# A hybrid encoder layer on one core: group 1's values and gates as seven block products, its weight sums made in group 0's retention stage, down-projection units 14 and 15 made ahead

## The chip, the core and the metric

The kernel runs on one core of a Trainium2 chip. Its time is the device time of one execution in microseconds (us); the number to compare is the median over several executions. The engines are TensorE (PE: matrix products; PEld is its weight load, which overlaps), VectorE (DVE), ScalarE (ACT), GpSimd (POOL) and SyncE (SP), which issues most of the transfers between DRAM and on-chip memory.

## The reference

One layer is applied to 2048 prompt frames and 8 streams of 16 new frames, all of width 1024. Its two token mixers share one input projection:

```python
p = jnp.einsum('btd,de->bte', x, w_in)
rq, rk, rv, rg, sq, sk, sv = jnp.split(p, PROJ_OFFSETS, axis=-1)
# retention: 4 heads, 128 wide
scores = jnp.einsum('bnhd,bmhd->bhnm', q, k) * dmask
o = jnp.einsum('bhnm,bmhe->bnhe', scores, v)
o = o + jnp.einsum('bnhd,bhde->bnhe', q, s) * q_decay[None, :, :, None]
return (jax.nn.silu(g.astype(jnp.float32)) * on).astype(g.dtype)   # on: o, normalised per head
# window attention: 8 query heads, 2 key heads, 64 wide, a sink in each softmax
p = sink_softmax(s, sinks)
o = jnp.einsum('bcgrqk,bckgd->bcqgrd', p.astype(v.dtype), vb)
# then, with mix = concatenate([retention, window attention])
x = layer_norm(ALPHA * x + jnp.einsum('btm,md->btd', mix, w_out), ln1_w, ln1_b)
h = jnp.square(jax.nn.relu(jnp.einsum('btd,df->btf', x, w_up)))
return layer_norm(ALPHA * x + jnp.einsum('btf,fd->btd', h, w_down), ln2_w, ln2_b)
```

The change concerns the columns `rv` and `rg` (values and gates of retention, 512 each) for six of the token tiles. Everything is computed to float32 accuracy.

## The kernel before

**Tiles, groups, stages.** The tokens stand in 17 tiles of 128, in three groups: group 0 has tiles 0 to 4, group 1 tiles 5 to 10, group 2 the sample tile and tiles 11 to 15. The groups run one after the other, each through stages whose names end the names of all buffers: keys and values of window attention (`1kv` for group 1), retention queries and keys (`1qk`; in group 0 a stage `0sq` instead), retention (`1ret`: values, gates, the recurrence), the output projection (`1out`) and the MLP (`1mlp`).

**Products.** [...] A product takes three matmuls: high by high, low by high, high by low. Where a weight is made into such a pair on the chip, ACT casts the high part (L297) and DVE subtracts to get the low part (L313).

**Seven block products.** Many projections go by a scheme of Strassen's kind: tokens are taken in pairs of half-blocks (three pairs of tiles in a group of six), the weight in 2 x 2 blocks, and seven products of sums of blocks stand for eight. Products are called 11, 12, 22 and S1 to S4; S1 to S4 of the weights are sums of weight blocks, T1 to T4 are the sums of the tokens that they meet (T2 meets S2, T1 meets S1, T3 meets S3, and T4 meets 22). Results are put together by DVE additions from PSUM. Before, queries and keys go this way in groups 1 and 2, values and gates (vg) only in group 2: `VGT = (2,)` at L54. In group 1 each of six tiles meets both halves of the 1024 value and gate columns directly: 2 x 6 x 8 slices x 3 = 288 matmuls of 128x512.

**The weight sums of vg.** `vg_operands` (L708) loads four blocks of the raw weight at a time, makes four sums on DVE (128x256 each), casts them on ACT, subtracts on DVE, and stores them in DRAM, in eight rounds. Before, it starts in group 1's MLP once that is past its first pair of units, one sum in 8 us. `vg_units` (from L2440) runs the seven products, in the order 11, 12, S2, S3, 22, S1, S4 (L413), with the stored sums reloaded as weights.

**The token sums.** `sums_task` (L1110) makes T1 to T4 for queries and keys. Where vg uses the seven products too, `store_sum` (L1092) saves T1 and T2 in DRAM before their room is given away, and `again_task` (L1101) reloads them in the retention stage.

**Down projection.** It has 16 units, used in pairs in the MLP. Group 0 makes their operands in place. For groups 1 and 2 `right_operands` (L756) can make units ahead and store them (kept_d), in the order 0, 1, 14, 15, 2, 3 and on; what isn't made ahead is made directly inside group 1's MLP (`direct_operand` L865, `direct_unit` L878), which also stores it for group 2. In this kernel units 0, 1, 14 and 15 are made ahead.

**Window attention.** `swa_task` (L1320) takes the prompt tiles of a group one by one: scores on TensorE, softmax on DVE and ACT, transposes of the probabilities on TensorE, copies, and the weighted sum on TensorE. In groups 1 and 2 the tiles from the fourth on go first. The output stage uses a tile's mix only when this is done; its units are taken by L2371 in the order of tiles 0, 3, 4, 5, 1, 2 for the first half of the columns in group 1.

**What sets the order.** The program is written by a planner (`Sched`, L58). Each piece of work is a generator that yields the time at which it wants to go on; a table of costs gives each engine's time, and TensorE's products are emitted in turn, with the pieces put between them as they come due. `idle("DVE", slack)` waits until the planner has DVE free; `room(tag, n)` waits for free buffers of a pool (14 of xT, 10 of w, 4 of raw, 20 of y, 8 of u3, 2 of st). So a change in one stage moves the order around it. Once written, the order on each engine is fixed. Transfers are issued by SP in the program's order, and each piece waits on semaphores for its inputs.

Of the kernel before, what the change touches and what calls it, by code (L numbers as in the profile page):

```python
# [11 lines left out]
ALU = mybir.AluOpType  # L12
# [41 lines left out]
VGT = (2,)  # L54
# [125 lines left out]
def tile_layer(ctx: ExitStack, tc: tile.TileContext, A: dict, O: dict):  # L180
# [527 lines left out]
    def vg_operands():  # L708

        while at_pair[0] < 1.0 or ph[0] != "1mlp":  # L710
            yield S.now + 1.0
# [8 lines left out]
        due = 0.0  # L720
        for n_ in range(8):
            kt, i = n_ // 2, n_ % 2
            while not room("y", 3):
                yield S.now + 0.3
            src = [take("y", [P, 2, 256]) for _ in range(2)]
# [4 lines left out]
            yield S.ready(*src) + 1.5  # L730
            a11, a12, a21, a22 = [src[x // 2][:, x % 2, :] for x in range(4)]
            for o, t, args in (("S1", a22, (a21, a22, ALU.add)), ("S3", a21, (a11, a21, ALU.subtract)),
                               ("S2", a11, (a22, a11, ALU.subtract)), ("S4", a12, (a12, a11, ALU.subtract))):
                while not room("y") or S.now < due:
                    yield S.now + 0.3
                due = S.now + 8.0
                hl = take("y", [P, 512], F32R)
                yield max(S.ready(*src, eng="DVE"), S.fence[hl.tensor.name])
                yield from idle("DVE", QUIET)
                vtt(t, *args)  # L740
                yield S.ready(t, eng="ACT")
                acopy(hl[:, 0:256], t)
                yield S.ready(hl[:, 0:256], eng="DVE")
                vtt(hl[:, 256:512], t, hl[:, 0:256].bitcast(F32), ALU.subtract)
                stored.append(S.add(save(kt, i, o, hl)))
# [10 lines left out]
    def right_operands():  # L756
# [43 lines left out]
        for n_, j in enumerate((0, 1, max(STR) - 2, max(STR) - 1) + tuple(range(2, max(STR) - 2))):  # L800
# [291 lines left out]
    def store_sum(o, hl, norms):  # L1092
        while not all(t[3] for t in norms):
            yield S.now + 0.5
        yield S.ready(*hl, eng="SP") - 0.3
        for k, t in zip(kept_t[o], hl):
            dma(k, t.bitcast(F32))

    norms = []
# [222 lines left out]
    def swa_task(tiles, slot, sq_tasks, qTs, kTall, vall, mixs, after=()):  # L1322
# [4 lines left out]
        if after:  # L1327
            todo.sort(key=lambda x: x[0] < 3)
# [732 lines left out]
    for gi, tiles in enumerate(GROUPS):  # L2061
# [102 lines left out]
        def qk_units(gi):  # L2164
# [40 lines left out]
            X = {"11": (0, 0), "12": (0, 1), "S4": (1, 1)}  # L2205
            for o, h in qk_order(gi):
                hs = [h_ for o_, h_ in qk_order(gi) if o_ == o]
# [587 lines left out]
        if not gi:  # L2795
            S.add(right_operands())
            if VGT:
                S.add(vg_operands())
# [192 lines left out]
```

## Time and profile before

| what | before |
|---|---|
| median of 3 runs | 2244.03 us (2242.72 to 2244.43) |
| profiled execution | 2241.79 us, span 2240.0 us |
| TensorE busy | 2221.1 us of the span |
| DVE busy | 1636.8 us |
| ACT busy | 1021.9 us |
| group 1: qk, retention, output | 95.13, 109.30 and 79.45 us |
| group 0: retention | 157.69 us |
| group 1: MLP | 467.71 us |

The stages' bounds are the first matmuls of TensorE whose results bear the stage's name. In rows of the profile, `out<-in` are buffers by the program's names with their numbers left out, L278 is the matmul helper, L284 the transposes, L297 ACT's copies and casts, L313 DVE's additions and subtractions, L359 the transfers. The time in brackets at a row's end is idle time before it, with the engine and the buffer that ended it.

### The profile page before, as it was taken

What the parts mean: (1) busy time and instruction counts of PE and PEld (TensorE: products, weight loads), DVE (VectorE), ACT (ScalarE), POOL (GpSimd) and SP (SyncE); (2) the same over time, 40 slices, a digit from 0 to 9 for tenths busy, and PEclk for the clock granted to TensorE, in tenths of its full rate; (3) what the DMA queues carried; (4) which work ended last, traced back from release to release, by engine and by line L of the source; (5) the groups of instructions that cost most, each with busy time, mean ns of one, the idle gap of its engine ahead of it and who ended that gap; (6) DMA issues with size and microseconds to landing.
All of it is one profiled execution on the core that took longest, in us unless ns stands there. A gap on an engine that the chain in (4) does not pass through costs nothing. (4 is left out here: it accounts for less than half of the span.)

```text
span 2240.0 us, 34600 instructions
## 1 busy us (share of the span) xinstructions
PE 2221.1 (99%) x12149; PEld 1969.8 (88%) x12149; DVE 1636.8 (73%) x3564; ACT 1021.9 (46%) x2407; POOL 95.8 (4%) x131
## 2 busy tenths in 40 slices
PE   9999999999999999999999999999999999999998
PEld 7788889999999988789999999899778999999987
DVE  6767689787877587787788887796775955555567
ACT  5544645555545555473344443366343732222222
POOL 0000000000000001000000000000000000000002
PEclk9999999999999999999999999999999999999999
DMA  7645758999989836767899998999655577777776
GB/s 263 213 169 211 284 197 306 319 327 341 322 311 352 289 130 221 258 247 252 286 338 333 334 336 302 330 346 354 237 172 183 178 254 256 249 252 257 254 255 179
DMA packets 228830, 598.91 MB, mean 267 GB/s; under 512 B 23216, under 2 KB 80304, under 8 KB 228656
## 3 DMA queue, kind: packets, MB, share of 16 engines
q1 hardware_dynamic: 223472, 587.26, 74.8%
q0 software_dynamic: 5184, 9.44, 2.5%
q8 instruction: 96, 1.57, 0.3%
q14 instruction: 78, 0.64, 0.1%
HBM read 401.25 MB, written 185.86 MB: 262 GB/s over the span
## 5 line engine op out<-in xcount | busy, mean ns | idle before, releaser
L278 PE MATMUL sw_1mlp<-xT_1out,w_1mlp 128*128 128x384 f32 x1152 | 209.2, 335 | 0.0
L278 PE MATMUL sw_2mlp<-xT_2out,w_2mlp 128*128 128x384 f32 x1140 | 206.8, 335 | 0.3 <-DVE kvln_2mlp L313 0.3
L278 PEld LDWEIGHTS sw_1mlp<-xT_1out,w_1mlp 128*128 128x128 f32 x1152 | 202.2, 188 | 4.1 <-DMA w_1mlp<-kept 0.5
L278 PEld LDWEIGHTS sw_2mlp<-xT_2out,w_2mlp 128*128 128x128 f32 x1140 | 200.0, 188 | 4.2 <-DVE kvln_2mlp L313 0.6
L278 PE MATMUL sw_0mlp<-xT_0out,w_0mlp 128*128 128x320 f32 x1188 | 179.1, 309 | 0.0
L278 PEld LDWEIGHTS sw_0mlp<-xT_0out,w_0mlp 128*128 128x128 f32 x1188 | 176.5, 188 | 2.2
L278 PE MATMUL rt_2mlp<-w_2mlp,u_2mlp 128*128 128x512 f32 (+1 forms) x522 | 127.1, 388 | 0.0
L278 PE MATMUL rt_1mlp<-w_1mlp,u_1mlp 128*128 128x512 f32 x516 | 126.8, 391 | 0.0
L278 PE MATMUL rt_0mlp<-w_0mlp,u_0mlp 128*128 128x512 f32 x492 | 121.3, 392 | 1.5 <-DVE u_0mlp L313 1.4
L278 PE MATMUL mm_2mlp<-w_2mlp,u_2mlp 128*128 128x512 f32 (+1 forms) x504 | 122.5, 388 | 0.0
L278 PE MATMUL mm_1mlp<-w_1mlp,u_1mlp 128*128 128x512 f32 x492 | 121.2, 391 | 0.0
L278 PEld LDWEIGHTS rt_2mlp<-w_2mlp,u_2mlp 128*128 128x128 f32 x522 | 96.9, 188 | 19.0
L278 PEld LDWEIGHTS rt_1mlp<-w_1mlp,u_1mlp 128*128 128x128 f32 x516 | 96.5, 188 | 19.2
L278 PE MATMUL mm_0mlp<-w_0mlp,u_0mlp 128*128 128x512 f32 x456 | 112.0, 392 | 0.0
L278 PEld LDWEIGHTS rt_0mlp<-w_0mlp,u_0mlp 128*128 128x128 f32 x492 | 92.2, 189 | 20.8 <-DVE u_0mlp L313 1.9
L278 PEld LDWEIGHTS mm_2mlp<-w_2mlp,u_2mlp 128*128 128x128 f32 x504 | 93.6, 188 | 18.4
L278 PEld LDWEIGHTS mm_1mlp<-w_1mlp,u_1mlp 128*128 128x128 f32 x492 | 92.0, 188 | 18.3
L278 PEld LDWEIGHTS mm_0mlp<-w_0mlp,u_0mlp 128*128 128x128 f32 x456 | 85.6, 189 | 17.2
L313 DVE TENSOR_TENSOR w_1mlp<-w_1mlp,w_1mlp 128x512 fp32r<-128x512 f32 (+1 forms) x120 | 81.7, 686 | 14.9 <-ACT w_1mlp L297 14.0
L313 DVE TENSOR_TENSOR w_0mlp<-raw_0mlp,w_0mlp 128x512 fp32r<-128x512 f32 (+1 forms) x69 | 63.5, 921 | 34.8 <-ACT w_0mlp L297 18.9
L297 ACT CAST u_2mlp<-kvln_2mlp 128x384 fp32r<-128x384 f32 x51 | 26.2, 515 | 117.7 <-PE mm_2mlp L278 52.1
L297 ACT CAST w_1mlp<-w_1mlp 128x512 fp32r<-128x512 f32 x84 | 52.0, 619 | 50.1 <-PE sw_1mlp L278 40.1
(1007 smaller groups left out, 4814.3 us busy)
## 6 DMA issues: line engine op xcount, KB each, us to landing
w_1mlp<-kept SPq DMA_DIRECT2D x104, 512.0 KB, 5.4
w_2mlp<-kept SPq DMA_DIRECT2D x102, 512.0 KB, 4.0
w_2mlp<-keptd SPq DMA_DIRECT2D x98, 512.0 KB, 4.2
kept<-w_0mlp SPq DMA_DIRECT2D x96, 512.0 KB, 5.1
keptd<-w_1mlp SPq DMA_DIRECT2D x84, 512.0 KB, 4.4
keptq<-y_0mlp SPq DMA_DIRECT2D x72, 256.0 KB, 5.1
w_1qk<-keptq SPq DMA_DIRECT2D x34, 512.0 KB, 5.7
w_2qk<-keptq SPq DMA_DIRECT2D x34, 512.0 KB, 6.2
```

The lines of the kernel that those rows point to most:

```text
L278: S.run("PE", lambda: nc.tensor.matmul(out, lhsT, rhs, start=start, stop=stop, skip_group_check=again), [out], [lhsT, rhs], cost)
L297: S.run("ACT", lambda: nc.scalar.copy(out, in_), [out], [in_], 0.06 + 0.83e-3 * size(out))
L313: S.run("DVE", lambda: nc.vector.tensor_tensor(out, a, b, op), [out], [a, b], dcost(out))
```

## The change

`VGT` becomes `(1, 2)`: group 1's values and gates are computed by the seven products over three pairs of tiles, 7 x 3 x 4 x 3 = 252 matmuls of 128x512, with 21 additions from PSUM behind them. `vg_operands` starts in group 0's retention stage, at the fifth tile of its first head, takes its buffers from the pools u3 and y, and loads each round's blocks ahead. T1 and T2 of group 1 are now saved in qk as soon as S1 or S2 is reached there, and reloaded in retention. `right_operands` takes units 14 and 15 first, begins at product S2 of group 1's vg, and gets no further than these two; units 0 and 1 are made inside group 1's MLP. `swa_task` keeps the tiles' own order in group 1, and the output units go in the order 0 to 5.

```diff
--- before.py
+++ after.py
@@ -51,7 +51,7 @@
-VGT = (2,)
+VGT = (1, 2)
@@ -707,8 +707,6 @@
     def vg_operands():
 
-        while at_pair[0] < 1.0 or ph[0] != "1mlp":
-            yield S.now + 1.0
         stored = []
...
-        due = 0.0
-        for n_ in range(8):
-            kt, i = n_ // 2, n_ % 2
-            while not room("y", 3):
-                yield S.now + 0.3
-            src = [take("y", [P, 2, 256]) for _ in range(2)]
+        def load(kt, i):
+            src = [take("u3", [P, 2, 256]) for _ in range(2)]
             for x in range(4):
                 g_ = 4 * (x % 2) + kt
                 o = 512 * (g_ % 2) + 256
                 dma(src[x // 2][:, x % 2, :], A["wret"][2 * (x // 2) + i, g_ // 2][:, o:o + 256])
-            yield S.ready(*src) + 1.5
+            return src
+
+        yield from wait_room("u3", 2)
+        ahead = load(0, 0)
+        for n_ in range(8):
+            src, hls = ahead, []
+            yield S.ready(*src) + 1.0
             a11, a12, a21, a22 = [src[x // 2][:, x % 2, :] for x in range(4)]
-            for o, t, args in (("S1", a22, (a21, a22, ALU.add)), ("S3", a21, (a11, a21, ALU.subtract)),
-                               ("S2", a11, (a22, a11, ALU.subtract)), ("S4", a12, (a12, a11, ALU.subtract))):
-                while not room("y") or S.now < due:
+            todo = (("S1", a22, (a21, a22, ALU.add)), ("S3", a21, (a11, a21, ALU.subtract)),
+                    ("S2", a11, (a22, a11, ALU.subtract)), ("S4", a12, (a12, a11, ALU.subtract)))
+            for o, t, args in todo:
+                yield from idle("DVE", 0.6)
+                vtt(t, *args)
+            for o, t, args in todo:
+                while not room("y", 2) and not room("u3", 5):
                     yield S.now + 0.3
-                due = S.now + 8.0
-                hl = take("y", [P, 512], F32R)
-                yield max(S.ready(*src, eng="DVE"), S.fence[hl.tensor.name])
-                yield from idle("DVE", QUIET)
-                vtt(t, *args)
-                yield S.ready(t, eng="ACT")
-                acopy(hl[:, 0:256], t)
+                hls.append(take("y" if room("y", 2) else "u3", [P, 512], F32R))
+                yield max(S.ready(t, eng="ACT"), S.fence[hls[-1].tensor.name])
+                acopy(hls[-1][:, 0:256], t)
+            if n_ < 7:
+                while not room("u3", 6):
+                    yield S.now + 0.3
+                ahead = load((n_ + 1) // 2, (n_ + 1) % 2)
+            for (o, t, args), hl in zip(todo, hls):
                 yield S.ready(hl[:, 0:256], eng="DVE")
+                yield from idle("DVE", 0.6)
                 vtt(hl[:, 256:512], t, hl[:, 0:256].bitcast(F32), ALU.subtract)
-                stored.append(S.add(save(kt, i, o, hl)))
+                stored.append(S.add(save(n_ // 2, n_ % 2, o, hl)))
...
-        for n_, j in enumerate((0, 1, max(STR) - 2, max(STR) - 1) + tuple(range(2, max(STR) - 2))):
+        for n_, j in enumerate((max(STR) - 2, max(STR) - 1, 0, 1) + tuple(range(2, max(STR) - 2))):
...
     def store_sum(o, hl, norms):
-        while not all(t[3] for t in norms):
+        while {'T2': 'S2', 'T1': 'S1'}[o] not in reached:
             yield S.now + 0.5
...
-    norms = []
+    norms, reached = [], set()
...
         todo = [(ti, t) for ti, t in enumerate(tiles) if t != SAMPLE]
-        if after:
+        if after and SAMPLE in tiles:
             todo.sort(key=lambda x: x[0] < 3)
...
+            reached.clear()
             for o, h in qk_order(gi):
+                reached.add(o)
...
-        units = [(0, ti) for ti in ((0, 3, 4, 5, 1, 2) if gi == 1 else (1,0,2,3,4,5) if gi in VGT else (0, 1, 2, 4, 3, 5))[:n]] + [(1, ti) for ti in ((4, 0, 2, 1, 3) if n == 5 else (0, 1, 2, 4, 3, 5))]
+        units = [(0, ti) for ti in ((0,1,2,3,4,5) if gi == 1 else (1,0,2,3,4,5) if gi in VGT else (0, 1, 2, 4, 3, 5))[:n]] + [(1, ti) for ti in ((4, 0, 2, 1, 3) if n == 5 else (0, 1, 2, 4, 3, 5))]
...
             for o in VG:
+                if o == "S2":
+                    begun[0] = True
                 if o == "S4":
...
+                    if gi == 0 and h0 == 0 and ti == 4:
+                        S.add(vg_operands())
...
             S.add(right_operands())
-            if VGT:
-                S.add(vg_operands())
...
             S.add(norm_end(ln2_tasks, lw + lb))
+            norms[:] = ln2_tasks
```

Three places show what this does to the order. In these rows a buffer's number follows its name, and `x2` at a row's end counts equal rows; a line of dots leaves out rows.

**TensorE where group 1's retention begins.** `rt_1qk` are the last products of qk, `sw_1ret` with columns of 192 the scores of window attention, `mm_1ret` the products of values and gates. Before, the scores of the second tile to be attended come first, then the products:

```order
L278 MATMUL rt_1qk_8948<-xT_1qk_8596,w_1qk_8776 128x384
L278 MATMUL rt_1qk_8948<-xT_1qk_8595,w_1qk_8776 128x384
L278 MATMUL sw_1ret_9094<-kvln_1kv_7957,raw_1qk_8675 128x192
L278 MATMUL sw_1ret_9095<-kvln_1kv_7957,raw_1qk_8675 128x192
...
L278 MATMUL sw_1ret_9101<-kvln_1kv_7957,raw_1qk_8675 128x192
L278 MATMUL mm_1ret_9088<-w_1qk_8823,xT_0mlp_7578 128x512
L278 MATMUL mm_1ret_9088<-w_1qk_8824,xT_0mlp_7578 128x512
L278 MATMUL mm_1ret_9088<-w_1qk_8823,xT_0mlp_7579 128x512
```

With the change nine products stand first, then the scores, which are those of the first tile:

```order
L278 MATMUL rt_1qk_9113<-xT_1qk_8807,w_1qk_8964 128x384
L278 MATMUL mm_1ret_9200<-w_1qk_8989,xT_0mlp_7786 128x512 x2
L278 MATMUL mm_1ret_9200<-w_1qk_8989,xT_0mlp_7787 128x512
L278 MATMUL mm_1ret_9200<-w_1qk_9021,xT_0mlp_7786 128x512 x2
L278 MATMUL mm_1ret_9200<-w_1qk_9021,xT_0mlp_7787 128x512
...
L278 MATMUL mm_1ret_9200<-w_1qk_9043,xT_0mlp_7787 128x512
L278 MATMUL sw_1ret_9220<-kvln_1kv_8165,y_1qk_8671 128x192
L278 MATMUL sw_1ret_9221<-kvln_1kv_8165,y_1qk_8671 128x192
...
L278 MATMUL mm_1ret_9200<-w_1qk_9067,xT_0mlp_7786 128x512 x2
L278 MATMUL mm_1ret_9200<-w_1qk_9067,xT_0mlp_7787 128x512
```

The products read token blocks of one pair of tiles with one weight after the other, and the first attention tile has moved out of qk into this stage.

**TensorE at the end of the fourth output unit of group 1.** `mm_1out` are the output unit's products, `sw_1out` from `cst` the transposes of the last tile's probabilities, `sw_1out` from `kvln_1kv` its weighted sum. Before:

```order
L278 MATMUL mm_1out_10527<-xT_1ret_10006,u_1out_10476 128x512
L284 MATMUL sw_1out_10543<-cst,u_1out_10372 128x128
...
L284 MATMUL sw_1out_10550<-cst,u_1out_10372 128x128 x4
L284 MATMUL sw_1out_10557<-cst,u_1out_10373 128x128 x4
L278 MATMUL mm_1out_10527<-w_1ret_10169,u_1out_10497 128x512
L278 MATMUL mm_1out_10527<-w_1ret_10170,u_1out_10497 128x512
...
L278 MATMUL mm_1out_10527<-w_1ret_10169,u_1out_10498 128x512
L278 MATMUL sw_1out_10577<-u_1out_10544,kvln_1kv_7958 64x256
L278 MATMUL sw_1out_10577<-u_1out_10545,kvln_1kv_7958 64x256
...
L278 MATMUL mm_1out_10527<-xT_1ret_10200,u_1out_10497 128x512
```

With the change:

```order
L278 MATMUL mm_1out_10675<-xT_1ret_10230,u_1out_10541 128x512
L284 MATMUL sw_1out_10720<-cst,u_1out_10592 128x128
...
L284 MATMUL sw_1out_10727<-cst,u_1out_10592 128x128 x4
L284 MATMUL sw_1out_10734<-cst,u_1out_10593 128x128 x4
L278 MATMUL sw_1out_10747<-u_1out_10721,kvln_1kv_8166 64x256
L278 MATMUL sw_1out_10747<-u_1out_10722,kvln_1kv_8166 64x256
...
L278 MATMUL sw_1out_10748<-u_1out_10722,kvln_1kv_8166 64x256
L278 MATMUL mm_1out_10766<-w_1ret_9966,u_1out_10669 128x512
```

The six products between transposes and weighted sum are gone from there; the next unit's products follow the weighted sum.

**DVE in group 0's retention.** `xT_0ret`, `tiny_0ret` and `state` belong to the recurrence and its normalisation, `y_0ret_1176` and `st_0ret` to other work of the stage. Before:

```order
L313 TENSOR_TENSOR y_0ret_1176<-y_0ret_1176,y_0ret_1175 128x512
L319 SCALAR_TENSOR_TENSOR xT_0ret_1681<-rt_0ret_1717,tiny_0ret_1765,xT_0ret_1681 128x128
L323 TENSOR_SCALAR xT_0ret_1681<-xT_0ret_1681,tiny_0ret_1770 128x128
L319 SCALAR_TENSOR_TENSOR xT_0ret_1752<-rt_0ret_1801,cst 128x128
L313 TENSOR_TENSOR st_0ret_1778<-y_0ret_1176,st_0ret_1777 128x512
L343 BN_STATS tiny_0ret_1856<-rt_0ret_1801 128x6
```

With the change:

```order
L313 TENSOR_TENSOR y_0ret_1176<-y_0ret_1176,y_0ret_1175 128x512
L319 SCALAR_TENSOR_TENSOR xT_0ret_1689<-rt_0ret_1725,tiny_0ret_1783,xT_0ret_1689 128x128
L323 TENSOR_SCALAR xT_0ret_1689<-xT_0ret_1689,tiny_0ret_1788 128x128
L313 TENSOR_TENSOR y_0ret_1744<-u_0ret_1561,y_0ret_1744 128x256
L313 TENSOR_TENSOR y_0ret_1746<-u_0ret_1561,y_0ret_1746 128x256
L313 TENSOR_TENSOR y_0ret_1748<-u_0ret_1560,y_0ret_1748 128x256
L313 TENSOR_TENSOR y_0ret_1757<-u_0ret_1560,y_0ret_1757 128x256
L319 SCALAR_TENSOR_TENSOR xT_0ret_1770<-rt_0ret_1819,cst 128x128
L313 TENSOR_TENSOR st_0ret_1796<-y_0ret_1176,st_0ret_1795 128x512
```

Four low parts of weight sums (`y_0ret` from `u_0ret`, 128x256) have come in between the operations on one head's result and the next.

## The prediction

> **What bounds the kernel now.** I read the page's busy shares first, then the stage windows, then what TensorE waits for.
>
> ```profile
> span 2240.0 us, 34600 instructions
> ...
> PE 2221.1 (99%) x12149; PEld 1969.8 (88%) x12149; DVE 1636.8 (73%) x3564; ACT 1021.9 (46%) x2407; POOL 95.8 (4%) x131
> ```
>
> TensorE (PE) has work for 2221.1 of 2240.0 us; no other engine is near. Since a share is an average, the stages that the change touches come next. Each row is a stretch of the program (start and end in us, length, busy time by engine, TensorE clock, DMA share, GB/s): group 1's queries and keys (qk), its retention stage, its output stage; the same three of group 2 up to retention; group 0's retention; group 1's MLP.
>
> ```profile
> core 0: us, PE busy (x) PEld busy (x) DVE busy (x) ACT busy (x) POOL busy (x), PEclk, DMA share, GB/s
> 706.91:802.04 95.13, 93.39 (x552) 90.53 (x550) 62.06 (x137) 56.20 (x123) 0.00 (x0) 1.00 0.89 305
> 802.04:911.34 109.30, 108.24 (x666) 88.49 (x666) 75.62 (x249) 51.55 (x174) 8.40 (x10) 1.00 0.46 167
> 911.34:990.79 79.45, 79.11 (x406) 64.50 (x404) 64.92 (x146) 50.16 (x114) 6.26 (x7) 1.00 0.69 247
> 1476.09:1565.58 89.49, 89.49 (x525) 88.91 (x524) 67.86 (x160) 59.84 (x139) 4.53 (x6) 1.00 0.95 348
> 1565.58:1690.89 125.31, 123.53 (x855) 95.67 (x855) 99.15 (x313) 53.82 (x199) 10.72 (x20) 1.00 0.61 206
> ...
> 60.89:218.58 157.69, 156.88 (x852) 127.96 (x851) 115.77 (x349) 73.84 (x222) 12.33 (x19) 1.00 0.55 189
> 990.79:1458.50 467.71, 467.10 (x2370) 424.91 (x2369) 367.91 (x667) 197.99 (x397) 0.86 (x1) 1.00 0.90 315
> ```
>
> In each, TensorE lacks under 2 us of being busy throughout, at a granted clock of 1.00. Group 1's retention, where the seven products come in, has 1.1 us without a matmul in 109.3. What it waits for in group 1's three stages, the largest first:
>
> ```profile
> PE sw_1qk L278 <- DVE raw_1qk L313: 1.2, 1, 1.2
> PE rt_1ret L278 <- ACT xT_1ret L293: 1.1, 2, 0.8
> PE sw_1qk L284 <- DVE u_1qk L313: 0.6, 2, 0.4
> ```
>
> So a matmul taken out of this stage is worth its own interval, and anything new that makes TensorE wait is paid in full. Both ledgers follow.
>
> **Matmuls removed.** The order of the program on TensorE has 288 products of 128x512 for group 1's values and gates before, and 252 after (7 products x 3 pairs of tiles x 4 slices x 3 terms); 36 go. Their price is the interval between starts in an undisturbed run of the same products:
>
> ```profile
> 802.04 1.57 PE L278 MATMUL sw_1ret<-kvln_1kv,raw_1qk 64*128 64x192 f32 x16
> 803.54 6.46 PE L278 MATMUL mm_1ret<-w_1qk,xT_0mlp 128*128 128x512 f32 x27
> 809.84 0.38 PE L284 MATMUL rt_1ret<-cst,xT_1qk 128*128 128x128 f32 x2
> ```
>
> (809.84 - 803.54) / 27 = 0.233 us; 36 x 0.233 = **8.4 us**. The mean of 0.4 us that groups print counts the overlap of pipelined matmuls and would say 14. The smallest price that a row supports is one weight load, 188 ns:
>
> ```profile
> L278 PEld LDWEIGHTS sw_1mlp<-xT_1out,w_1mlp 128*128 128x128 f32 x1152 | 202.2, 188 | 4.1 <-DMA w_1mlp<-kept 0.5
> ```
>
> 36 x 0.188 = 6.8 us, the other bound. I take 8.4, because the rows are of the very products. [...]
>
> **Window attention starts later.** The scores, softmax and weighted sum of each tile are a chain through DVE and ACT, which TensorE's order interleaves. Before, the first tile is done inside qk, with two of the waits above:
>
> ```profile
> 779.68 0.59 PE L278 MATMUL sw_1qk<-kvln_1kv,raw_1qk 64*128 64x192 f32 x4
> 781.47 1.25 PE L278 MATMUL sw_1qk<-kvln_1kv,raw_1qk 64*128 64x192 f32 x12 [1.19 <-DVE raw_1qk L313]
> ...
> 799.71 1.68 PE L278 MATMUL sw_1qk<-u_1qk,kvln_1kv 128*64 128x256 f32 x16
> ```
>
> After, the first scores stand behind nine value products of the retention stage. Its matmuls cost the same wherever they stand; the two waits (1.2 + 0.6 us) have lost their place. Some seventy matmuls later, the rotated queries that the first was short of should be long there. I take -1.2, with 0 (the wait appears in front of the next chain) and -1.8 as bounds.
>
> The chain now has to end sooner after it starts. In the output stage, the last tile's transposed probabilities are copied out of PSUM before its weighted sum; before, six matmuls cover this:
>
> ```profile
> 937.11 1.47 PE L284 MATMUL sw_1out<-cst,u_1out 128*128 128x128 f32 x12
> 938.33 1.64 PE L278 MATMUL mm_1out<-w_1ret,u_1out 128*128 128x512 f32 x6
> 939.90 1.68 PE L278 MATMUL sw_1out<-u_1out,kvln_1kv 128*64 128x256 f32 x16
> ```
>
> and ACT's copies run from 938.18 to 939.25:
>
> ```profile
> 938.18 1.07 ACT L297 COPY u_1out<-sw_1out 128x512 f32<-128x512 f32 x2 [3.20 <-PE sw_1out L284]
> ```
>
> After, the weighted sum follows the transposes directly, and the fifth output unit with the rest of the stage is queued behind it on TensorE. The transposes end at about 938.3 on that clock and the copies 0.9 to 1.1 us behind: **+1.1**. Below, 0, if what DVE and ACT do ahead of the copies shrinks; above, 4.3, if the softmax ahead of the transposes is late too: the row shows that ACT stood 3.2 us waiting for TensorE, and 1.1 + 3.2 is paid if that slack turns into its opposite.
>
> **DVE in group 0's retention.** The sums of weight blocks move from group 1's MLP into this stage: 64 DVE operations and 32 casts on ACT. Their prices as they stand today:
>
> ```profile
> L313 DVE TENSOR_TENSOR w_1mlp<-w_1mlp,w_1mlp 128x512 fp32r<-128x512 f32 x84 | 57.6, 686 | 14.1 <-ACT w_1mlp L297 14.0
> ...
> L313 DVE TENSOR_TENSOR y_1mlp<-y_1mlp,y_1mlp 128x256 fp32r<-128x256 f32 x32 | 13.4, 419 | 1.7 <-ACT y_1mlp L297 1.7
> ...
> L313 DVE TENSOR_TENSOR y_1mlp<-y_1mlp 128x256 f32<-128x256 f32 x16 | 6.7, 418 | 0.5 <-DMA y_1mlp<-in_wret_dram 0.5
> L313 DVE TENSOR_TENSOR y_1mlp<-y_1mlp,y_1mlp 128x256 f32<-128x256 f32 x16 | 6.7, 418 | 0.0
> ```
>
> 13.4 + 6.7 + 6.7 = 26.8 us. The stage has 157.69 - 115.77 = 41.9 us of DVE free, so it fits, at 90% busy. But they come in fours, 4 x 0.42 = 1.7 us at a time, ahead of the short operations of the recurrence that TensorE's next transposes wait for. Today this stage shows one such wait:
>
> ```profile
> PE rt_0ret L284 <- DVE xT_0ret L323: 0.8, 1, 0.8
> ```
>
> I take one more of it, **+0.8**; bounds 0 (the planner asks for an idle DVE before each) and 3.2 (0.2 us for each of the 16 batches). Their transfers move too: 32 loads of 0.13 MB and 32 stores of 0.26 MB are 12.6 MB, which make 269 GB/s of the stage's 189 and are needed only hundreds of microseconds later; group 2's qk moves 348 GB/s without a wait. Nothing for those.
>
> **DVE at the start of group 1's MLP.** Down-projection units 0 and 1 are no longer made ahead; their operands are formed inside the MLP from raw weights: 22 more additions of 512, 22 x 0.686 = 15.1 us, against the 26.8 that leave. Where they fall is the question. Two stretches of that MLP:
>
> ```profile
> 1040.00:1090.00 50.00, 50.00 (x253) 45.30 (x252) 29.20 (x52) 17.03 (x33) 0.00 (x0) 1.00 0.71 246
> 1010.00:1020.00 10.00, 10.00 (x59) 10.00 (x59) 9.93 (x19) 2.87 (x6) 0.00 (x0) 1.00 0.83 254
> ```
>
> From 1040 DVE has 20.8 us to spare in 50; around 1015 it has none, and the first pair of units is used just between. What comes late is the operand of unit 1's third product. Group 0, which makes all of its units in place, paid one wait at this spot:
>
> ```profile
> PE rt_0mlp L278 <- DVE u_0mlp L313: 1.4, 1, 1.4
> ```
>
> I take about a third of it, **+0.5**; bounds 0 and 3 (once for each unit).
>
> **Costed at nothing.** In group 1's retention 21 additions of 512 come and 20 operations of that size go (14 on loaded rows, 6 on results), 0.7 us net on a DVE with 33.7 us free: 0; bounds -1.1 (the wait on ACT there goes) and +1.5. In qk, four stores of the activation sums, 3.1 MB, come and two loads, 0.8 MB, go: 305 GB/s x 95.13 us = 29.0 MB becomes 31.3, or 329 GB/s. Group 2's qk moves 348 GB/s with TensorE busy 89.49 of 89.49 us, so 0. The sums' reload and 28 weight loads in retention meet a DMA share of 0.46; group 2's retention does the same work at 0.61, and its largest wait is for something else:
>
> ```profile
> PE rt_2ret L278 <- DMA y_2ret<-in_st_dram: 0.6, 2, 0.5
> ```
>
> If that cover fails, one late 0.5 MB load costs a wait of this size.
>
> **Sum.** -8.4 - 1.2 + 1.1 + 0.8 + 0.5 = -7.2 us. The profiled execution took 2241.79 us (1.8 beside its span), 2.2 below the median of the runs, so profiled 2234.6, and by the median **2236.8**. All lower ends: -8.4 - 1.8 - 1.1 = -11.3, 2232.7. All upper ends: -6.8 + 4.3 + 3.2 + 3 + 1.5 = +5.2, 2249.2.
>
> **The rivals.** *Late operands give the gain back.* Full DVE at both places, in retention of group 0 and the first pair of group 1's MLP, reaches its upper ends: -8.4 - 1.2 + 1.1 + 3.2 + 3 = -2.3, and **2241.7**. For it: DVE at 90% and 99%. Against: today's waits on DVE there sum to 0.8 us and less. 0.13.
>
> *The chain of window attention sets group 1's end (slower).* Six tiles take from 779.68 to 941.58, 27 us each. After, the first scores come at about 797 and the fifth output unit, behind the last tile in the order, is due at about 935, leaving 23 each. If a tile's softmax kept 27 us, the end would slip 6 x 4 = 24 us, of which the gain takes 8: **2260**; from 24.3 us per tile it eats the gain. For it: the chain's DVE and ACT steps are queued behind the new additions. Against: group 2 runs five tiles with the same products in
>
> ```profile
> 1559.27 1.57 PE L278 MATMUL sw_2qk<-kvln_2kv,raw_2qk 64*128 64x192 f32 x16
> ```
> ```profile
> 1670.20 1.68 PE L278 MATMUL sw_2ret<-u_2ret,kvln_2kv 128*64 128x256 f32 x16
> ```
>
> (1671.88 - 1559.27) / 5 = 22.5 us each, and the first tile above took 22. 0.06.
>
> *TensorE's busy time is not the bound.* If the stage had slack that the matmul rows hide, fewer matmuls only widen it: no change, **2244**. For it: weight loads fill just 88.49 of 109.30 us of group 1's retention. [...] Against: starts 0.233 us apart in a row of 27 with no wait between, longer than a load's 0.188, so the matmul itself sets the pace. 0.05.
>
> *Every wait in group 1 vanishes* and nothing new appears: -11, **2233**. 0.08.
>
> **How the numbers follow.** The forecast has 0.68, with its own range 2234 to 2239.5. No change within 0.2% means within 4.5 us of 2244.0, which is what a measurement of this kernel can tell; the forecast lies 2.7 us beyond that edge. Faster takes 0.67 of the forecast and the 0.08: 0.75. The same takes late operands and hidden slack: 0.18. Slower takes the chain, and the hundredth of the forecast in which all upper ends meet: 0.07. The range 2232.5 to 2243.5 takes in all of the lower ends and late operands, and leaves out hidden slack and the chain.
>
> **What would show it.** Group 1's three stages together should shrink by some 8 us; qk by about 6.5 (a tile's matmuls, 1.57 + 1.47 + 1.68 = 4.7 in the rows above, and the two waits), with the tile's 4.7 us back in the output stage. Behind the last tile's transposes TensorE should wait about 1 us for a copy by ACT. The forecast is wrong if group 0's retention grows by over 3 us, if the down products of group 1's first pair wait for DVE, if TensorE waits for w or xT tiles from DMA in group 1's retention, or if the wait for probabilities in its output stage is many us: then the term named there has to be re-sized.

## The result and the profile after

| | us | runs |
|---|---|---|
| before, median | 2244.03 (2241.47 to 2244.43) | 7 |
| with the change, median | 2236.31 (2234.99 to 2238.16) | 7 |
| ratio | 0.9970, 95% interval 0.9958 to 0.9981 | |
| predicted | 2236.8 (2232.5 to 2243.5) | |

The change takes 7.7 us between the medians. Run again beside the experiments it had 2236.01 against 2242.06 for the kernel before, a ratio of 0.9974 (0.9964 to 0.9984), so 6 to 8 us is what it is worth. The experiments below are set against these 2236.01; the kernel before, run beside them, lay between 2242.06 and 2242.20 each time. One execution of the run with the longer softmax chains, 2746.71 us at a granted clock of 0.75 where all others have 0.99 or more, is a slow one and is left out of its median.

The page of the profiled execution (2236.31 us) begins:

```profile
span 2234.5 us, 34503 instructions
...
PE 2213.7 (99%) x12113; PEld 1961.5 (88%) x12113; DVE 1648.9 (74%) x3585; ACT 1017.4 (46%) x2395; POOL 95.8 (4%) x131
```

TensorE has 36 instructions fewer, as the order said, and 7.4 us less work in a span that is 5.5 us shorter; 1.4 us of the 7.4 stand in group 0's MLP and come from the clock (see the early sums below). By stage (start and end, length, busy time by engine, TensorE clock, DMA share, GB/s): group 0's retention with its output stage, group 0's MLP, group 1's qk, its retention with its output stage, its MLP, and group 2's retention with its output stage.

```profile
62.01:269.75 207.74, 206.41 (x1081) 167.98 (x1080) 167.81 (x481) 110.59 (x307) 15.41 (x24) 1.00 0.78 268
269.75:690.57 420.82, 418.01 (x2318) 378.25 (x2316) 349.36 (x669) 229.24 (x492) 27.00 (x30) 1.00 0.90 304
708.27:796.26 87.99, 87.95 (x508) 87.56 (x507) 49.53 (x106) 47.87 (x96) 0.00 (x0) 1.00 0.95 351
796.26:985.70 189.44, 185.83 (x1081) 149.40 (x1081) 151.44 (x425) 102.24 (x295) 14.71 (x17) 1.00 0.57 201
985.70:1453.89 468.19, 466.77 (x2366) 424.50 (x2364) 358.69 (x619) 192.20 (x376) 0.86 (x1) 1.00 0.82 292
...
1560.97:1755.49 194.52, 193.34 (x1198) 153.70 (x1198) 146.17 (x421) 92.57 (x277) 16.38 (x27) 1.00 0.53 181
```

The same stretches of the kernel before, cut in the same way where the prediction did not show them:

```profile
60.89:267.58 206.69, 205.88 (x1081) 168.27 (x1080) 144.89 (x413) 102.00 (x281) 15.50 (x24) 1.00 0.59 208
267.58:689.20 421.62, 419.42 (x2317) 379.32 (x2316) 349.13 (x669) 228.50 (x490) 27.03 (x30) 1.00 0.90 304
...
802.04:990.79 188.75, 187.34 (x1070) 153.00 (x1069) 140.54 (x394) 101.71 (x287) 14.66 (x17) 1.00 0.56 200
990.79:1458.49 467.70, 467.09 (x2369) 424.91 (x2368) 367.91 (x667) 197.99 (x397) 0.86 (x1) 1.00 0.90 315
...
1565.58:1760.87 195.29, 193.51 (x1198) 153.82 (x1197) 146.03 (x421) 92.57 (x277) 16.28 (x27) 1.00 0.53 181
```

Group 1's qk falls by 7.1 us: one tile of window attention has left it, and its 1.74 us of idle TensorE became 0.04. Retention and output together took that tile in, gave up 36 matmuls, and end 0.7 us longer; over the three stages 283.9 us became 277.4 (276.5 in the profile of the second run of the change), 6.4 or 7.4 less where the prediction said some 8. Group 0's retention and output pay 1.05 us, group 1's MLP 0.5; group 0's MLP and group 2's retention are each 0.8 shorter. In group 1, from qk to the start of the MLP, TensorE now waits for:

```profile
PE mm_1out L278 <- DMA w_1out<-halves_out: 1.2, 2, 0.7
PE mm_1mlp L278 <- ACT y_1mlp L297: 0.9, 1, 0.9
PE sw_1out L284 <- DVE u_1out L313: 0.7, 2, 0.5
PE sw_1ret L278 <- DVE y_1qk L313: 0.6, 1, 0.6
PE mm_1mlp L278 <- ACT y_1mlp L293: 0.5, 1, 0.5
PE mm_1ret L278 <- ACT y_1ret L297: 0.5, 1, 0.5
PE rt_1ret L278 <- ACT xT_1ret L293: 0.3, 1, 0.3
PE sw_1out L278 <- ACT u_1out L297: 0.2, 1, 0.2
```

The waits in qk are gone, the one on retention's xT has shrunk from 1.1 to 0.3, and seven are new. The largest, for output weights from DRAM, is in no term of the prediction.

### The profile page after: what moved, and what is told of

Same layout as the page of the kernel before. It is cut to its first block, busy times and chain, and to the rows that moved or that the text cites. A ratio compares the mean times of both kernels' runs of the same rounds, so it can differ in the third digit from the quotient of the medians.

```text
span 2234.5 us, 34503 instructions
## 1 busy us (share of the span) xinstructions
PE 2213.7 (99%) x12113; PEld 1961.5 (88%) x12113; DVE 1648.9 (74%) x3585; ACT 1017.4 (46%) x2395; POOL 95.8 (4%) x131
## 5 line engine op out<-in xcount | busy, mean ns | idle before, releaser
L278 PE MATMUL sw_0mlp<-xT_0out,w_0mlp 128*128 128x320 f32 x1152 | 173.9, 309 | 0.0
L278 PEld LDWEIGHTS sw_0mlp<-xT_0out,w_0mlp 128*128 128x128 f32 x1152 | 171.2, 188 | 2.2
L313 DVE TENSOR_TENSOR w_1mlp<-w_1mlp,w_1mlp 128x512 fp32r<-128x512 f32 (+1 forms) x140 | 95.7, 688 | 19.7 <-ACT w_1mlp L297 18.7
L297 ACT CAST w_1mlp<-w_1mlp 128x512 fp32r<-128x512 f32 x98 | 60.7, 620 | 76.2 <-PE sw_1mlp L278 67.0
```

Of the source, the lines that this page charges most:

```text
L278: S.run("PE", lambda: nc.tensor.matmul(out, lhsT, rhs, start=start, stop=stop, skip_group_check=again), [out], [lhsT, rhs], cost)
L297: S.run("ACT", lambda: nc.scalar.copy(out, in_), [out], [in_], 0.06 + 0.83e-3 * size(out))
L313: S.run("DVE", lambda: nc.vector.tensor_tensor(out, a, b, op), [out], [a, b], dcost(out))
```

## The experiments

**What a matmul is worth.** The first two runs put matmuls back without touching the order of anything else.

```diff
+    extra = [0]
...
     def mm3(ps, lh, ll, rh, rl, first, last, again=False):
         S.pump()
+        for _ in range(extra[0]):
+            nc.tensor.matmul(ps, lh, rh, start=True, stop=False, skip_group_check=True)
+        extra[0] = 0
         matmul(ps, lh, rh, first, False, again)
...
+                        if gi == 1 and not kt:
+                            extra[0] = 1 * (1 if o in ("S1", "S4") else 2)     # 36; with 3 *: 108
                         mm3(ps, xh, xl, wh, wl, kt == 0, kt == 3)
```

> The changed kernel with 36 matmuls of 128x512 added back: in group 1's values and gates the first matmul of a product's sum is issued twice (three times in five of the seven products); the later one overwrites the earlier, so the result stays. Theory A (TensorE sets the pace, a matmul is worth its own interval): 36 x 0.233 = +8.4 us on the changed kernel, about 2244.7, level with before. If a matmul is worth a weight load only (0.188): +6.8, about 2243. Rival (hidden slack: the removed matmuls were free and the gain came from the other edits): no change, about 2236.3.

> The same with three times as many copies, 108. Theory A: +25.2 us, about 2261.5, and three times the step of the run with 36. At 0.188 us a piece: +20.3, about 2256.6. Rival (hidden slack): the first few tens of matmuls are free and only the rest shows, so the step is clearly less than in proportion.

Measured: 2244.69 us with 36 (1.0010 of before, 1.0001 to 1.0019) and 2260.94 with 108 (1.0079, 1.0066 to 1.0092). From the changed kernel that is 8.7 us for 36, 0.24 us each, and 24.9 for 108, 0.23 each; between the two runs, 16.25 / 72 = 0.226. No first part of the step is free. Group 1's retention and output stages in the two runs:

```profile
796.33:991.77 195.44, 193.20 (x1117) 156.39 (x1117) 151.33 (x425) 102.10 (x295) 14.72 (x17) 1.00 0.55 195
```
```profile
798.23:1009.85 211.62, 209.40 (x1190) 169.92 (x1189) 151.54 (x425) 102.25 (x295) 14.72 (x17) 1.00 0.51 180
```

In these two stages the 36 add 6.0 us to the changed kernel's 189.44 (7.0 to the 188.49 of its second profile) and the 108 add 22.2. TensorE's listed waits there fall from 3.5 us to 2.1 in both runs, so a few of the added matmuls only fill waits. Between the two runs, whose waits are alike, 72 matmuls add 16.2 us, 0.225 each. The rest of the longer spans is not theirs: in the profile with 36, group 2's retention is 4.5 us longer, behind a transfer that came 2.0 us late; in that with 108, group 1's qk starts 2.0 us later than in the changed kernel's (710.24 against 708.27). How much of the like is in the medians is not known; by the intervals above, 8.7 is good to about 3 us. Hidden slack is refuted all the same, and with it the reading that 79% of weight-load occupancy (149.40 of 189.44) leaves room for more.

With its 36 matmuls back, the changed kernel is 2.5 us slower than before, not level. So the products earn 8 to 9 us and the other edits cost about 2.5, each good to 2 or 3 us. The next two runs take those apart.

**The other edits alone.** First all of them without the products:

```diff
-VGT = (1, 2)
+VGT = (2,)
```

> All edits but the seven products: group 1's values and gates go directly again (288 matmuls), with the weight sums made in group 0's retention, the new orders of attention tiles, output units and units made ahead kept. Theory A: the edits bring nothing by themselves; +0.8 us for DVE in group 0's retention and up to 2 for the new orders: 2244 to 2247. Rival (the gain is in the moves): 2236 to 2239.

Measured: 2244.88 us, 1.0011 of before (1.0002 to 1.0020), which is +2.7. The moves bring nothing by themselves. That this is close to the 2.5 of the first run is in part chance, since the order written anew differs from the changed kernel's in more than the products: three units are made ahead (six loads of `in_wdn_dram` before the MLP, two for a unit; the changed kernel has four), no token sums of group 1 are stored, and TensorE waits 2.7 us for output weights where the changed kernel waits 1.2.

Then only the early weight sums, in the kernel before (`vg_operands` with its new body, started at group 0's fifth tile):

```diff
+                    if gi == 0 and h0 == 0 and ti == 4:
+                        S.add(vg_operands())
...
             S.add(right_operands())
-            if VGT:
-                S.add(vg_operands())
```

> The kernel before with one edit: the weight sums are made in group 0's retention stage, as in the changed kernel, and no longer in group 1's MLP. Theory A: +0.8 us (0 to 3.2) in that stage and nothing gained in group 1's MLP: about 2244.8. Rival (late operands: a DVE at 90% there holds up the recurrence): +3 us, about 2247. A gain in group 1's MLP, where the work leaves, would show as under 2243.

Measured: 2243.06 us against 2242.20, 1.0003 (0.9994 to 1.0012): +0.9 with an interval that holds zero. The profile is sharper; group 0's retention and output, its MLP, and group 1's MLP:

```profile
62.02:269.72 207.70, 206.36 (x1081) 167.99 (x1080) 167.66 (x481) 110.69 (x307) 15.46 (x24) 1.00 0.78 269
269.72:690.50 420.78, 417.99 (x2317) 378.24 (x2316) 349.25 (x669) 229.10 (x492) 27.04 (x30) 1.00 0.89 304
992.29:1459.72 467.43, 466.86 (x2370) 425.07 (x2368) 348.91 (x606) 184.06 (x358) 0.86 (x1) 1.00 0.80 287
```

The first two lengths are those of the changed kernel within 0.04 us: +1.0 in retention and output, -0.8 in the MLP behind. The +1.0 belongs to the early sums, the -0.8 does not. In group 0's MLP TensorE waits 1.4 us for `u_0mlp` in both kernels; in the profile before, it then ran at half clock (0.50 in the clock column) for 3.4 us, and in the changed kernel's profile it did not. The stretch behind that wait, before and with the change:

```profile
301.66:305.07 3.41, 3.41 (x10) 2.63 (x9) 2.98 (x6) 0.00 (x0) 0.00 (x0) 0.50 0.11 44
```
```profile
304.65:308.06 3.41, 3.41 (x17) 2.81 (x16) 3.41 (x8) 0.00 (x0) 0.00 (x0) 1.00 0.10 39
```

From the end of that wait, 43 matmuls of 128x512 take 11.51 us before (301.05 to 312.56) and 9.89 with the change (304.03 to 313.92). That prices the stretch at 1.6 us, and the kernel before would take an estimated 420.0 without it. So the early sums cost about 0.8 us in this MLP too: TensorE waits 0.8 us there for DVE's `xT_0out`, which before it did not. Taking the sums out of group 1's MLP gains 0.3 there.

**How near to the edge is DVE in group 0's retention?** A second helping of the same work, with TensorE's order unchanged:

```diff
                 yield from idle("DVE", 0.6)
+                for _ in range(2):
+                    nc.vector.tensor_tensor(hl[:, 256:512], t, hl[:, 0:256].bitcast(F32), ALU.subtract)
                 vtt(hl[:, 256:512], t, hl[:, 0:256].bitcast(F32), ALU.subtract)
```

> The changed kernel with each of the 32 subtractions of low parts in group 0's retention issued three times (the later ones overwrite with the same values): 64 more DVE operations of 0.42 us, 26.8 us, in the same places; TensorE's order is the same. DVE is now busy 135.2 of 158.2 us there, so this asks for more than the stage has. Theory (the move was near the edge: it cost 1 us and a second helping costs several): +3 to +10 us on the changed kernel, with TensorE waiting for DVE's xT and state in that stage. Rival (DVE has cover enough there, the 1 us is not of DVE): 0 to +1 us.

Measured: 2262.69 us, +26.7 on the changed kernel, far over the expectation. The stage, and what TensorE waits for in it:

```profile
62.24:245.82 183.58, 166.70 (x852) 132.87 (x851) 159.54 (x466) 83.66 (x250) 12.27 (x20) 0.95 0.68 229
```
```profile
PE rt_0ret L278 <- DVE xT_0ret L319: 7.7, 5, 2.6
PE rt_0ret L284 <- DVE xT_0ret L313: 6.2, 2, 3.3
PE rt_0ret L284 <- DVE xT_0ret L323: 2.2, 2, 1.4
```

The first 26.8 us of DVE work cost 1 us in retention and output, and the next 26.8 cost 25.4 in retention alone (158.20 before the dose). DVE is idle for 24 us of the longer stage all the same: operations of the recurrence that TensorE needs stand behind a batch in DVE's queue. Of the 25.4 us, TensorE stands for 16.0 more (16.9 without a matmul, 0.9 before the dose), and the same 852 matmuls take 9.4 more, at a mean clock of 0.95. So an estimated 11 of the 26.8 us still found cover, and the slower clock in this stage makes the rest dear. The mechanism of the rival "late operands" is real; the change itself stopped short of it.

**Half of the sums on GpSimd.**

```diff
-            for o, t, args in todo:
-                yield from idle("DVE", 0.6)
-                vtt(t, *args)
+            for o, t, (a, b, op) in todo:
+                S.run("POOL", lambda: nc.gpsimd.tensor_tensor(t, a, b, op), [t], [a, b], 0.13 + 2.3e-3 * 256)
+                yield S.now + 0.1
```

> The changed kernel with the 32 sums of weight blocks in group 0's retention on GpSimd in place of DVE (the 32 subtractions of low parts stay): DVE has 13.4 us less to do there, in batches half as many; the planner's order changes a little. Theory (DVE's batches cost the 1 us): -0.5 us on the changed kernel, retention and output of group 0 together 207.2 where they are 207.7. Rival (the cost lies elsewhere, in transfers or ACT's casts): no change, or slower if GpSimd is late.

Measured: 2239.04 us, +3.0 and not -0.5. Group 0's retention and output take 210.27 us, with DVE less busy:

```profile
60.70:270.97 210.27, 207.36 (x1081) 167.86 (x1080) 162.29 (x446) 111.76 (x312) 41.64 (x56) 1.00 0.76 264
```

TensorE waits longer for DVE there all the same (2.6 us in three waits, 1.2 in two in the changed kernel). The mean duration of two groups of DVE operations (behind the bar: busy us, mean ns), in this run and then in the changed kernel:

```profile
L313 DVE TENSOR_TENSOR xT_0ret<-xT_0ret 128x128 f32<-128x128 f32 x40 | 11.2, 321 | 0.7
L313 DVE TENSOR_TENSOR st_0ret<-y_0ret,st_0ret 128x512 fp32r<-128x512 f32 x14 | 10.4, 744 | 0.0
```
```profile
L313 DVE TENSOR_TENSOR xT_0ret<-xT_0ret 128x128 f32<-128x128 f32 x40 | 9.9, 288 | 0.7
L313 DVE TENSOR_TENSOR st_0ret<-y_0ret,st_0ret 128x512 fp32r<-128x512 f32 x14 | 9.6, 685 | 0.0
```

Both groups are longer in the run with the sums on GpSimd (288 to 321 ns, 685 to 744); a third, which takes one input from a product's result (`xT_0ret` from `mm_0ret`, 128x256), is not, 418 ns there and 419 in the changed kernel. Which part of the 3 us is that, and which the planner's other order, this run doesn't separate.

**Units 14 and 15 or 0 and 1.**

```diff
-        for n_, j in enumerate((max(STR) - 2, max(STR) - 1, 0, 1) + tuple(range(2, max(STR) - 2))):
+        for n_, j in enumerate((0, 1, max(STR) - 2, max(STR) - 1) + tuple(range(2, max(STR) - 2))):
```

> The changed kernel with one edit undone: units 0 and 1 of the down projection are made ahead again, and 14 and 15 inside group 1's MLP. TensorE's order is the same up to the end of that MLP. Theory (operands made in place are late for the first pair): the waits of 0.9 and 0.5 us on ACT at the start of group 1's MLP go, and that MLP falls from 468.35 us to about 467.5; the last pair gets no wait, since DVE has time there: -0.6 us on the changed kernel. Rival (those waits come from elsewhere, or move to the last pair): no change.

Measured: 2266.30 us, 1.0108 of before (1.0094 to 1.0122), 30.3 us slower than the changed kernel. The two waits of 0.9 and 0.5 us at the first pair are gone, as expected: they do come from units 0 and 1 made in place. But the operands of the last pair come late. The largest wait in group 1's MLP, and then the largest behind it, where group 2 begins:

```profile
PE mm_1mlp L278 <- ACT w_1mlp L297: 3.8, 1, 3.8
```
```profile
PE rt_2kv L284 <- ACT kvln_2kv L297: 5.7, 1, 5.7
PE sw_2kv L278 <- ACT xT_1mlp L297: 5.7, 1, 5.7
PE sw_2kv L278 <- DVE xT_1mlp L313: 4.4, 3, 2.6
```

Group 2's stage of keys and values needs its tokens split by ACT and DVE, and in DVE's order those splits stand behind the operands of 14 and 15, the last sums of the MLP and its norms. It takes 44.07 us in place of 17.6, at a clock of 0.69:

```profile
1455.57:1499.64 44.07, 26.18 (x150) 23.80 (x148) 41.83 (x100) 27.45 (x73) 4.30 (x6) 0.69 0.80 299
```

So the edit to `right_operands` is no trifle: with two units made ahead, which two is worth 30 us.

**The old order of attention and output units.**

```diff
-        if after and SAMPLE in tiles:
+        if after:
             todo.sort(key=lambda x: x[0] < 3)
...
-        units = [(0, ti) for ti in ((0,1,2,3,4,5) if gi == 1 else (1,0,2,3,4,5) if gi in VGT else (0, 1, 2, 4, 3, 5))[:n]] + [(1, ti) for ti in ((4, 0, 2, 1, 3) if n == 5 else (0, 1, 2, 4, 3, 5))]
+        units = [(0, ti) for ti in ((0, 3, 4, 5, 1, 2) if gi == 1 else (1,0,2,3,4,5) if gi in VGT else (0, 1, 2, 4, 3, 5))[:n]] + [(1, ti) for ti in ((4, 0, 2, 1, 3) if n == 5 else (0, 1, 2, 4, 3, 5))]
```

> The changed kernel with the old order of window attention (tiles from the fourth on first) and of output units (0, 3, 4, 5, 1, 2) in group 1. Theory (the new order is needed by the products, whose values for the fourth to sixth tile come last): the second output unit waits for tile 3's retention, +2 to +5 us on the changed kernel, though attention starts inside the queries-and-keys stage again. Rival (the new order is what costs: the waits of 2 us behind the last tile's transposes and 0.6 at the first scores): -2 us.

Measured: 2254.13 us, 1.0057 (1.0045 to 1.0070), 18.1 us slower than the changed kernel. The mechanism is the expected one, at more than three times the upper end: TensorE waits for retention's results, which the old order wants sooner. The two orders were not tried apart.

```profile
PE rt_1ret L278 <- ACT xT_1ret L293: 4.5, 1, 4.5
PE rt_1out L284 <- DVE xT_1ret L323: 3.9, 1, 3.9
```

**Is the chain of window attention near its limit?** More work on each of the six tiles, first within the chain:

```diff
+                    for _ in range(2 if t in GROUPS[1] else 0):
+                        nc.vector.tensor_reduce(mx[:, 4 * c + 2 * g:4 * c + 2 * g + 2], ps[g], axis=AX.X, op=ALU.max)
                     vmax(mx[:, 4 * c + 2 * g:4 * c + 2 * g + 2], ps[g])
```

> The changed kernel with each maximum of the softmax of window attention in group 1 taken three times: 8 more DVE operations of 0.5 us in each of the six tiles, 4 us on each tile's chain; TensorE's order is the same. Theory (the order leaves the first five tiles cover, only the last tile's probabilities are awaited): about +4 us on the changed kernel, all behind the last tile. Rival of the prediction (the chain of six tiles sets the end of group 1): +24 us, 4 for each tile.

Measured: 2272.37 us, +36.4. My theory (+4) falls, and the size is the rival's or more. But the waits are not attention's:

```profile
PE rt_1ret L278 <- ACT xT_1ret L293: 4.8, 2, 4.6
PE rt_1ret L284 <- DVE y_1ret L323: 4.0, 1, 4.0
PE rt_1ret L284 <- DVE xT_1ret L323: 4.0, 1, 4.0
```

These, and three more of 2.8 to 3.8 us, are waits for steps of the retention stage, most of them late by nearly the estimated 4.4 us that one tile's eight extra reductions take (0.55 us each in the changed kernel's profile). So a last run put the same eight reductions behind the tile's last step on DVE, where attention's chain does not feel them:

```diff
                     vtt(pb[g][:, :, sl], pb[g][:, :, sl], r, ALU.mult)
+            for g in range(2):
+                for _ in range(4 if t in GROUPS[1] else 0):
+                    nc.vector.tensor_reduce(mx[:, 2 * g:2 * g + 2], pb[g][:, :, 0:192], AX.X, ALU.max)
```

> The changed kernel with the same dose as in the run before, 8 DVE reductions of 0.5 us for each of group 1's six attention tiles, but issued behind the tile's last step on DVE, on results that nobody reads: the chain of attention is no longer, DVE's queue is. Theory (the queue: what stands behind a block on DVE, the normalisation of retention's heads, is late by it, whatever the block is for): six stalls of nearly 4 us again, +20 to +37 us on the changed kernel. Rival (the chain: only attention's own steps were late): 0 to +4 us.

Measured: 2266.62 us, +30.6. Attention's own wait stays at 0.7 us; TensorE waits for retention again:

```profile
PE rt_1ret L278 <- ACT xT_1ret L293: 5.2, 3, 4.1
PE rt_1out L278 <- ACT xT_1ret L293: 4.3, 1, 4.3
PE rt_1ret L284 <- DVE xT_1ret L323: 3.5, 1, 3.5
```

So the queue alone makes most of this cost: what TensorE needs from DVE waits for whatever stands in front of it. From 797 to 990 us TensorE has 21.9 us without a matmul, where retention and output in the changed kernel have 3.6 (its waits for output weights grow from 1.2 to 3.1 us on the way), and the mean clock there is 0.94. Why the run with the reductions inside the chain costs 6 us more was not taken apart. That DVE is busy for 79.8 of 100.6 us of this stage says nothing on how much more it takes in one piece.

**The late output weights.** The wait that the prediction lacked can be removed. In the changed kernel the first half's output weights fill the w buffers, so half of the second half's are issued at the last moment; they may go into xT buffers instead:

```diff
-                spare += [("xT", 6)] if key[1:3] == ("out", 0) else [("xT", 5)] if key[1] == "sq" else []
+                spare += [("xT", 2 if key[0] == 1 else 6)] if key[1:3] == ("out", 0) else [("xT", 5)] if key[1] == "sq" else []
```

> The changed kernel with one more edit: in group 1 the output weights of the first half may be loaded into xT buffers when only two of these are free (six before), so that w buffers are left for the second half. Theory (the waits for w_1out at the seventh output unit, 1.2 us with 1.7 of lost intervals, come from weights issued late for want of w buffers): these waits go, -1.2 to -1.7 us on the changed kernel. Rival (transfers are slow there whenever they are issued): no change, or a wait for another transfer.

> The changed kernel itself once more, on the chip of the next three, so that they can be set against it. Both theories: 0.997 of before, about 6.5 us under it.

Measured on the same chip: 2234.48 us (0.9967 of before, 0.9955 to 0.9980) and 2236.01 for the change itself (0.9974). The waits for w_1out are gone from its list, as is the one of 0.5 us for ACT's `y_1mlp`; the largest that stay, from group 1's output on:

```profile
PE mm_1mlp L278 <- ACT y_1mlp L297: 0.8, 1, 0.8
PE sw_1out L284 <- DVE u_1out L313: 0.7, 2, 0.5
```

So want of w buffers is what made these weights late. The 1.5 us between the two are of the expected size, though the intervals overlap, and in the profiles the gain stands half elsewhere: retention and output are 0.8 us shorter (187.67 against 188.49), and group 1's MLP 1.0. By its median it is the fastest version that was run.

## Why the prediction was right, point by point

- **Matmuls removed: right.** 36 at 0.233 made 8.4; added back, they cost 0.23 to 0.24 each by the medians and 0.225 by the stage between the two runs, 8.1 to 8.7 in all. A weight load's 0.188 is too low.
- **Attention starts later: right.** -1.2 predicted: qk's 1.8 us of waits went, and 0.6 came back in front of the first scores, for queries that the prediction thought long there. (Its "some seventy matmuls" between the old and the new place are 96 by TensorE's order.)
- **The last tile's wait: sized at half of what came.** +1.1 predicted behind the transposes, for ACT's copy. The listed wait there is 0.2; another 0.7 stands ahead of the transposes, for DVE's normalised probabilities:

```profile
931.40 0.30 PE L284 MATMUL sw_1out<-cst,u_1out 128*128 128x128 f32 x1 [0.48 <-DVE u_1out L313]
931.87 1.39 PE L284 MATMUL sw_1out<-cst,u_1out 128*128 128x128 f32 x11 [0.17 <-DVE u_1out L313]
933.50 2.44 PE L278 MATMUL sw_1out<-u_1out,kvln_1kv 128*64 128x256 f32 x16 [0.24 <-ACT u_1out L297]
```

By the starts the cost is higher. The next product starts at 935.86, so transposes and weighted sum take 4.5 us where the rows before give 1.2 and 1.6, and the transposes start some 0.7 us late: 2.3 us in all. The bound of 4.3 named a late softmax, the value taken did not.
- **DVE in group 0's retention: sized at less than half.** +0.8 predicted. Retention and output grew by 1.05 us, and the MLP behind them by an estimated 0.8, which the profile before hides under its stretch at half clock. (The stretch of 157.69 us given for this retention ends 11 us behind the first output product, which starts at 207.52. Up to that product the stage takes 146.64 us, and 147.15 with the change, so half of the 1.05 stands in the output stage.)
- **DVE at the start of group 1's MLP: the size right by luck.** +0.5 predicted, 0.49 measured, but as a balance: two new waits of 0.9 and 0.5 came, one of 0.6 for the stage's tokens went, and the sums that left gave 0.3. The run with units 0 and 1 ahead ties the new waits to these units. The full DVE is behind them, one step away: TensorE waits for ACT, which had waited for DVE. But what comes late is not "the operand of unit 1's third product"; it is ACT's reading of a product's result (`y_1mlp` from `mm_1mlp`), for which TensorE's next product waits:

```profile
1025.47 0.49 ACT L293 ACTIVATE y_1mlp<-mm_1mlp 128x384 f32<-128x384 f32 x1 [2.90 <-DVE u_1mlp L313]
```
```profile
1026.02 1.65 PE L278 MATMUL mm_1mlp<-w_1mlp,u_1mlp 128*128 128x512 f32 x6 [0.51 <-ACT y_1mlp L293]
```

The step also looked only at where the work goes. What the other half of that edit saves, units 14 and 15 at the end, was not costed, since before made them ahead too.
- **Costed at nothing: the step that failed.** The cover of the loads was argued from bandwidth, for qk and retention, and the output weights were in no term. They came late for want of w buffers, 1.2 us in one profile and 0.6 in another. In retention 0.5 for a copy by ACT came and 0.8 of the old wait there went.
- **The sum.** +1.2 us was forecast for all edits but the products, and about 2.5 was measured, good to about 2 us. With 8 to 9 for 8.4 on the other side: -7.2 forecast, -7.7 and -6.1 measured. For group 1's three stages alone the terms sum to -8.5, and the two profiles show -6.4 and -7.4. Since three terms were too small by a microsecond or more, that the total came so near is in part luck; which errors cancelled was not taken apart.
- **The rivals.** Hidden slack is refuted by the two doses. Late operands and the slower case, the chain, did not happen. The doses price them: another 27 us of DVE work in group 0 cost 27 us, and eight reductions in front of each tile's normalisation in group 1 cost 31 to 36. How much less would have set them off was not tried. The chain's price of 24 had about the right size, but what makes it is not attention's latency; it is what stands behind attention in DVE's queue.

## What to carry to other kernels

Where one engine is busy 99% of the time and waits are listed, the interval between starts in an undisturbed row prices each instruction that is added or removed; it held here (0.233 by the row, 0.225 between the two runs that add matmuls). Another engine's idle share priced nothing here: of the DVE work put into group 0's retention the first 26.8 us cost 1 us, and the next 26.8 cost 25.4, since they stood in front of what TensorE waits for, 9.4 of the 25.4 in matmuls that took longer at a mean clock of 0.95. So look at what is queued behind the place and how long a block it is. When a schedule is regenerated, also ask which buffers the new operands occupy, since the loads that wait for those buffers can come late though bandwidth is free (1.2 us of waits here, in stages that moved 201 GB/s where qk moved 351).

## What the runs showed of the hardware

In these runs a stall cost more than the stall: with the second helping of DVE work, 16.0 us more without a matmul came with 9.4 us of longer matmuls. In the profile of the kernel before, the last few microseconds aside, the clock granted to TensorE is 1.00 but for one stretch of 3.41 us at 0.50; in the changed kernel's it is 1.00 throughout. Two stretches at 0.50 from the run with units 0 and 1 ahead, the first behind a wait of 2.6 us, the second, seven times as long, beginning inside one of 5.7 and holding others:

```profile
1465.46:1468.87 3.41, 3.34 (x17) 3.08 (x15) 3.38 (x10) 2.14 (x9) 0.00 (x0) 0.50 1.03 400
```
```profile
1472.29:1496.18 23.89, 11.54 (x46) 10.07 (x47) 23.14 (x52) 17.57 (x43) 3.71 (x4) 0.50 0.61 208
```

A shorter wait stood ahead of one too. Before and with the change TensorE waits 1.4 us for `u_0mlp` in group 0's MLP; before, the 3.41 us at half clock follow, and with the change none do. What decides it these runs do not show. With the longer softmax chains, whose stalls are of some 4 us, TensorE has 24.7 us without a matmul in the 182.24 from 797.76 to 980, and in six of the eight windows that make up this time, of 20 to 40 us each, the mean clock is 0.83 to 0.92. A profile that is compared with another to a microsecond should therefore be searched for such stretches first.

Two groups of DVE's operations were about a tenth longer in the run with the sums on GpSimd (685 to 744 and 288 to 321 ns), which the prediction had not reckoned with, as it moved nothing there.
